# State-space SiLU as u/2 times (1 + tanh(u/2)), applied behind each convolution in a hybrid encoder step

## The chip, the cores and the metric

One Trainium2 chip; the kernel runs on one of its cores. The metric is device time in microseconds (us) of one launch, as the median of several runs. Engine names below: PE is TensorE (PEld its weight loads), DVE is VectorE, ACT is ScalarE, POOL is GpSimd, SP is SyncE.

## What is computed

One inference step of a hybrid encoder layer over 512 prompt frames and 64 sample frames, which the kernel handles together as T = 576 columns. The layer is a half SwiGLU feed-forward, a mixer, another half SwiGLU, and a final norm. The mixer has three branches: a state-space scan (SSD), band attention and an mLSTM. The change lies in the state-space branch:

```python
z, xbc, ... = split_cols(u @ lp['w_in'], IN_SIZES)
xbc, conv_new = causal_conv(xbc, conv_prev, lp['ssd_conv_w'], lp['ssd_conv_b'])   # width 4, per channel
xs, bm, cm = split_cols(jax.nn.silu(xbc), (SSD_WIDTH, SSD_GROUPS * SSD_STATE, SSD_GROUPS * SSD_STATE))
y, ssd_new = ssd_scan(xs, dt, a, bm, cm, h0)        # chunked scan, 16 heads in 4 groups
y = y + lp['ssd_d'][:, None] * xs
y_ssd = rmsnorm(y * jax.nn.silu(z), lp['ssd_norm'])
```

silu(v) is v times the logistic function of v. With u = v/2 it equals u times (1 + tanh(u)).

## The kernel before

Everything is kept with features on the 128 partitions and frames along the free axis. A matrix product is done in a split form (a rounded high part and a remainder, `ph` and `pl` for weights, `TH` and `TL` for activations; three products for one), with a seven-product scheme on 2 x 2 blocks: `stream` walks over blocks of weights, and each block gives seven products of 12 matmuls (`product`, L623). The weights come by DMA to `wr`, `wx` or are summed on POOL to `wy` (L479); `split` rounds them on ACT (L289, a cast) and takes the remainder on DVE (L290).

The mixer's projections run through `pairs`: two output tiles of 128 features at a time. A product's result lies in one of three accumulator banks; part of the results is first copied out by ACT to a temporary `uv` (L540), others are put in place by DVE together with a `uv` (L549), or by ACT alone (L547). A bank takes the next product only after that.

The mixer works in twelve units, `ORDER = a0 a1 m0 s0 a2 a3 s1 m1 s2 m2 s3 m3`: attention (a), mLSTM (m), state space (s). While the products of one unit stream through PE, the *job* of an earlier unit is woven in: each product calls `tick`, which advances a generator to its next `yield`. A unit's job is queued when its last product is done. So what a job emits is placed, in program order, among the products of the following unit. The order in which each engine finally issues its instructions isn't this order: a scheduler works it out from a simulated timeline, and each engine then runs its own list strictly in that order.

A state-space unit (`ssd_gemm`) has six tiles in three pairs: B and C, x0 and x1, z0 and z1. For B, C, x0, x1 the put function `conv` collects the two halves in a tile `raw` from a ring of four buffers (tag `P`, also used by attention and mLSTM jobs), copies three boundary columns out (L1156, L1157), and does the convolution: one ACT instruction (L1159, scale and bias) and three DVE instructions (L1162), into `acc` (a tile of tag `g`). z0 and z1 go to rows 0 and 1 of `R1`. The job (`ssd`) begins with its row loads by DMA (L182, L1182) and then applies the six SiLUs in a row (L1185, L1188), the first one before the others by `issue_after`. After that it multiplies B and C (L1197), turns B to frame-major order (`tok_major`, L906, L910) and x0, x1 likewise (L1226, L1230); x is weighted by `wd` on ACT (L1236), the decay matrices are formed on ACT (L1242 to L1245) and multiplied on POOL (L1246, L1247); then come the state chain and the outputs, the last with z (L1294, L1295).

ACT evaluates functions from a loaded table; the program has a table-load instruction (`ACT_TABLE_LOAD`) wherever a function is needed that the loaded set lacks. Exp and tanh are used all over the mixer, SiLU here and in the two feed-forwards.

Of the kernel before, what the change touches and what calls it, by code (L numbers as in the profile page):

```python
# [27 lines left out]
AF = mybir.ActivationFunctionType  # L28
ALU = mybir.AluOpType
# [29 lines left out]
C_CW = 48  # L59
C_CB = 112  # L60
# [21 lines left out]
class Hybrid:  # L82
# [1052 lines left out]
    def ssd_gemm(self, g):  # L1135
        nc = self.nc
        out = {}

        def conv(key, ct, col):
            box = {}  # L1140
            w = self.cst[:, C_CW + ct * 4:C_CW + ct * 4 + 4]

            def go(h, sl, emit):
                if not box:
                    box["raw"] = raw = self.P((128, 582))
                    nc.scalar.copy(raw[:, 0:3], self.zero)
                    nc.scalar.copy(raw[:, 515:518], self.cst[:, C_CS + ct * 3:C_CS + ct * 3 + 3])
                raw = box["raw"]
                m = min(sl.stop, TP)
                emit(raw[:, 3 + sl.start:3 + m], 0, m - sl.start)  # L1150
                if sl.stop > TP:
                    emit(raw[:, 6 + TP:6 + sl.stop], TP - sl.start, sl.stop - sl.start)
                box[h] = True
                if not (0 in box and 1 in box):
                    return
                nc.scalar.copy(self.co[:, ct, 0:3], raw[:, 512:515])  # L1156
                nc.scalar.copy(self.co[:, ct, 3:6], raw[:, 579:582])  # L1157
                acc = self.t("g", (128, 579))
                nc.scalar.activation(acc, raw[:, 0:579], AF.Identity, scale=w[:, 0:1],  # L1159
                                     bias=self.cst[:, C_CB + ct:C_CB + ct + 1])  # L1160
                for j in range(1, 4):
                    nc.vector.scalar_tensor_tensor(acc, raw[:, j:j + 579], w[:, j:j + 1], acc,  # L1162
                                                   op0=ALU.mult, op1=ALU.add)
                out[key] = acc
            return ("w_in", col), 1.0, go

        def zed(j, col):
            return ("w_in", col), 1.0, lambda h, sl, emit: emit(self.R1[:, j, sl])

        tiles = [conv("B", 8 + g, O_B + g * 128), conv("C", 12 + g, O_C + g * 128),  # L1170
                 conv("x0", 2 * g, O_X + g * 256), conv("x1", 2 * g + 1, O_X + g * 256 + 128),
                 zed(0, O_Z + g * 256), zed(1, O_Z + g * 256 + 128)]
        return tiles, out

    def ssd(self, g, t):
        nc = self.nc
        Bf, Cf = t["B"], t["C"]
# [4 lines left out]
                nc.scalar.dma_start(rows[j][2][r * 64:(r + 1) * 64, :], self.rows(4 * g + 2 * j + r, 64))  # L1182
        free = 2 + (self.b_i - 1) % 2 * 3

        last = nc.scalar.activation(self.R1[:, 0, :], self.R1[:, 0, :], AF.Silu)  # L1185
        with self.tc.issue_after(last.ins):
            for v in (Bf, Cf, t["x0"], t["x1"], self.R1[:, 1, :]):
                nc.scalar.activation(v, v, AF.Silu)  # L1188
        yield 2
        h4 = lambda ap: ap.rearrange("p c (h e) -> p c h e", e=64)  # L1190
        v4 = lambda ap: ap.rearrange("p (c t) -> p c t", t=128)
# [3 lines left out]
        for c in range(4):  # L1195
            sl = slice(c * 128, (c + 1) * 128)
# [10 lines left out]
        for j in range(2):  # L1207
# [7 lines left out]
            for r in range(2):  # L1215
                last = cum[r][:, 127:512:128]
# [37 lines left out]
            for c, (a, n) in enumerate(CH):  # L1254
# [9 lines left out]
                else:  # L1264
                    h = states[c]
                    for r in range(2):
                        hs = slice(r * 64, (r + 1) * 64)
                        nc.vector.scalar_tensor_tensor(new[:, hs], h[:, hs], el[:, c, r:r + 1], ps[:, hs],
                                                       op0=ALU.mult, op1=ALU.add)
# [73 lines left out]
    def merge(self):  # L1343
# [71 lines left out]
        half(1, (2, 3))  # L1415
        heads(7)
        ssd(range(2))
        half(2, (0, 1))
        ssd(range(2, 5))
        half(2, (2, 3))  # L1420
        ssd(range(5, 8))
        tiles = [(("w_proj_ssd", 0, 1024, n * 128, 128), [(0, put(n, 0))]) for n in range(8)]
        self.gemm(tiles[:4], ZH, ZL)
# [61 lines left out]

    def branches(self, x):
        nc = self.nc
        units = {"a": (self.attn_gemm, self.attn), "m": (self.ml_gemm, self.ml), "s": (self.ssd_gemm, self.ssd)}
        got = {u: units[u[0]][0](u[1]) for u in ORDER[:2]}
        with self.wide("m0"), self.pools("m0", xp=None, op=None):  # L1490
# [134 lines left out]
```

## Time and profile before

| | |
|---|---|
| runs | 1925.25, 1933.16, 1935.91 us; median 1933.16 |
| profiled execution (the page gives its span, and no other time for it) | 1934.5 us from the first to the last instruction |
| granted TensorE clock, mean | 0.992 |
| busy: PE, DVE, ACT, POOL | 97%, 79%, 56%, 35% of the span |
| table loads on ACT | 11 in all; 8 of them between 755 and 1147 us |

How to read it: the first feed-forward ends at about 550 us, the mixer lies between there and about 1365 us, and the second feed-forward fills the rest. The four state-space jobs begin at 755.7, 904.8, 1011.4 and 1116.9 us, where their first table load stands.

### The profile page before, as it was taken

What the parts mean: (1) busy time and instruction counts of PE and PEld (TensorE: products, weight loads), DVE (VectorE), ACT (ScalarE), POOL (GpSimd) and SP (SyncE); (2) the same over time, 40 slices, a digit from 0 to 9 for tenths busy, and PEclk for the clock granted to TensorE, in tenths of its full rate; (3) what the DMA queues carried; (4) which work ended last, traced back from release to release, by engine and by line L of the source; (5) the groups of instructions that cost most, each with busy time, mean ns of one, the idle gap of its engine ahead of it and who ended that gap; (6) DMA issues with size and microseconds to landing.
All of it is one profiled execution on the core that took longest, in us unless ns stands there. A gap on an engine that the chain in (4) does not pass through costs nothing. (4 is left out here: it accounts for less than half of the span.)

```text
span 1934.5 us, 37668 instructions
## 1 busy us (share of the span) xinstructions
PE 1884.4 (97%) x13901; PEld 1822.9 (94%) x13901; DVE 1525.9 (79%) x2715; ACT 1091.1 (56%) x2502; POOL 672.9 (35%) x644
## 2 busy tenths in 40 slices
PE   8999999999999999999999999999999999999998
PEld 8999999999999878888889989999999999999998
DVE  6999899988868767767777776745898988889765
ACT  5554654644534787767676766324565455554544
POOL 3433333333302234423535353450233333343311
PEclk9999999999999999999999999999999999999999
DMA  7266666666742545754666655672236666666631
GB/s 231 82 162 168 162 159 164 154 172 171 181 133 90 142 129 146 215 147 117 170 180 178 164 145 184 205 220 83 84 105 164 164 159 167 165 157 169 153 97 57
DMA packets 129439, 294.69 MB, mean 152 GB/s; under 512 B 14288, under 2 KB 26192, under 8 KB 129256
## 3 DMA queue, kind: packets, MB, share of 16 engines
q1 hardware_dynamic: 99496, 203.58, 32.5%
q0 software_dynamic: 20272, 74.20, 20.9%
q10 hardware_dynamic: 9488, 14.53, 2.5%
q8 instruction: 109, 1.79, 0.4%
q14 instruction: 74, 0.61, 0.1%
HBM read 272.87 MB, written 19.38 MB: 151 GB/s over the span
## 5 line engine op out<-in xcount | busy, mean ns | idle before, releaser
L623 PE MATMUL acc<-TH,ph 128*128 128x288 f32 x3220 | 966.7, 301 | 25.2 <-ACT uv L540 11.2
L623 PE MATMUL acc<-TL,ph 128*128 128x288 f32 x3220 | 954.1, 297 | 0.4 <-DVE TL L290 0.4
L623 PE MATMUL acc<-TH,pl 128*128 128x288 f32 x3220 | 952.5, 297 | 0.3 <-DVE pl L290 0.2
L623 PEld LDWEIGHTS acc<-TH,ph 128*128 128x128 f32 x3220 | 605.9, 188 | 45.2 <-ACT uv L540 14.7
L623 PEld LDWEIGHTS acc<-TL,ph 128*128 128x128 f32 x3220 | 607.3, 189 | 4.6 <-issue 3.7
L623 PEld LDWEIGHTS acc<-TH,pl 128*128 128x128 f32 x3220 | 606.6, 189 | 3.4 <-issue 2.0
L290 DVE TENSOR_TENSOR pl<-wr,ph 128x512 fp32r<-128x512 f32 x471 | 439.4, 940 | 89.1 <-ACT ph L289 76.8
L289 ACT CAST ph<-wr 128x512 fp32r<-128x512 f32 x471 | 286.7, 618 | 277.7 <-PE acc L623 140.7
L290 DVE TENSOR_TENSOR pl<-wx,ph 128x512 fp32r<-128x512 f32 x390 | 322.6, 831 | 38.8 <-ACT ph L289 32.6
L289 ACT CAST ph<-wx 128x512 fp32r<-128x512 f32 x390 | 236.9, 619 | 199.5 <-POOL wx L479 98.6
L479 POOL TENSOR_TENSOR wx<-wx,wr 128x512 f32<-128x512 f32 x160 | 243.6, 1522 | 181.7 <-DVE pl L290 147.0
L468 POOL DMA_DIRECT2D wx<-in_sblk x115 | 101.3, 898 | 504.8 <-DVE pl L290 156.8
L261 PE MATMUL acc<-YH,ph 128*128 128x256 f32 (+1 forms) x768 | 228.6, 299 | 2.5 <-ACT g L547 2.4
L261 PE MATMUL acc<-YL,ph 128*128 128x256 f32 (+1 forms) x768 | 229.0, 299 | 0.5
L261 PE MATMUL acc<-YH,pl 128*128 128x256 f32 (+1 forms) x768 | 229.3, 299 | 0.0
L261 PEld LDWEIGHTS acc<-YH,ph 128*128 128x128 f32 x768 | 147.0, 192 | 3.0 <-ACT g L547 2.6
L261 PEld LDWEIGHTS acc<-YL,ph 128*128 128x128 f32 x768 | 147.2, 192 | 1.6 <-DVE YL L340 1.5
L261 PEld LDWEIGHTS acc<-YH,pl 128*128 128x128 f32 x768 | 147.3, 192 | 0.0
L479 POOL TENSOR_TENSOR wy<-wx,wr 128x512 f32<-128x512 f32 x35 | 54.5, 1557 | 133.3 <-DVE pl L290 117.1
L662 DVE SCALAR_TENSOR_TENSOR R<-acc,R 128x288 f32<-128x288 f32 x168 | 75.5, 450 | 18.5 <-PE acc L623 17.9
L289 ACT CAST TH<-g 128x288 fp32r<-128x288 f32 x120 | 51.4, 434 | 54.8 <-POOL g L648 33.5
L290 DVE TENSOR_TENSOR pl<-wy,ph 128x512 fp32r<-128x512 f32 x70 | 61.3, 879 | 26.4 <-ACT ph L289 23.7
(321 smaller groups left out, 2386.4 us busy)
## 6 DMA issues: line engine op xcount, KB each, us to landing
wr<-in_sblk SPq DMA_DIRECT2D x345, 256.0 KB, 3.7
wx<-in_sblk POOLq DMA_DIRECT2D x119, 512.0 KB, 6.8
wx<-in_sblk SPq DMA_DIRECT2D x111, 512.0 KB, 3.8
wr<-in_wblk SPq DMA_DIRECT2D x126, 256.0 KB, 3.0
R<-scr_rows ACTq DMA_DIRECT2D x12, 576.0 KB, 5.7
gs<-g SPq DMA_DIRECT2D x20, 288.0 KB, 4.3
g<-gs POOLq DMA_DIRECT2D x20, 288.0 KB, 3.5
y<-ys POOLq DMA_DIRECT2D x12, 288.0 KB, 4.5
```

The lines of the kernel that those rows point to most:

```text
L261: nc.tensor.matmul(ps[:, :n], wt[:, wsl], xx[:, k0 + k, a:a + n], start=(k == 0 and i == 0), stop=(k == nk - 1 and i == 2))
L289: self.nc.scalar.copy(hi, src)
L290: self.nc.vector.tensor_tensor(lo, src, hi.bitcast(F32), op=ALU.subtract)
L468: return {"x12": x12, "src": src}, lambda: nc.gpsimd.dma_start(x12, src[:, 1:3, :], accum_op=ALU.add)
L479: add = lambda o, one, two: self.nc.gpsimd.tensor_tensor(o, one, two, op=ALU.add)
L623: self.nc.tensor.matmul(ps, wt[:, wsl], xx[:, kk, :], start=(start and kk == 0 and i == 0), stop=(kk == 3 and i == 2), skip_group_check=True)
L662: self.nc.vector.scalar_tensor_tensor(o, ps, scale, o, op0=ALU.mult, op1=ALU.add)
```

## The change

SiLU goes from ACT's SiLU function in the job to a tanh and one DVE instruction where the tile is finished. `silu_of_half(u, t)` writes tanh(u) to t (ACT, L1185 of the new file) and then u = (t + 1) * u (DVE, L1186). For B, C, x0, x1 it stands right behind the three convolution instructions and writes the tanh into `raw`, which stays taken so much longer. For z0 and z1 it stands behind the second half and takes a buffer of the `P` ring that was not taken before. The halving of u is put in the constants: one POOL instruction at the start of `branches` halves the convolution's weights and bias, and z's scale is 0.5 instead of 1.0. The six SiLUs of the job are gone.

```diff
                 for j in range(1, 4):
                     nc.vector.scalar_tensor_tensor(acc, raw[:, j:j + 579], w[:, j:j + 1], acc,
                                                    op0=ALU.mult, op1=ALU.add)
+                self.silu_of_half(acc, raw[:, 0:579])
                 out[key] = acc
...
         def zed(j, col):
-            return ("w_in", col), 1.0, lambda h, sl, emit: emit(self.R1[:, j, sl])
+            seen = []
+            def go(h, sl, emit):
+                emit(self.R1[:, j, sl])
+                seen.append(h)
+                if len(seen) == 2:
+                    self.silu_of_half(self.R1[:, j, :], self.P())
+            return ("w_in", col), 0.5, go
...
+    def silu_of_half(self, u, t):
+        self.nc.scalar.activation(t, u, AF.Tanh)
+        self.nc.vector.scalar_tensor_tensor(u, t, 1.0, u, op0=ALU.add, op1=ALU.mult)
...
-        last = nc.scalar.activation(self.R1[:, 0, :], self.R1[:, 0, :], AF.Silu)
-        with self.tc.issue_after(last.ins):
-            for v in (Bf, Cf, t["x0"], t["x1"], self.R1[:, 1, :]):
-                nc.scalar.activation(v, v, AF.Silu)
...
+        half = self.cst[:, C_CW:C_CB + 16]
+        nc.gpsimd.tensor_scalar(half, half, 0.5, None, op0=ALU.mult)
```

The table loads in the program fall from 11 to 3. Line numbers of the new file are 9 to 11 higher behind the change (L1197 becomes L1206, L1236 becomes L1245, L1242 to L1245 become L1251 to L1254). Since the scheduler orders each engine's list anew, instructions move in the whole stage. Three places show it.

ACT where unit s2's products end and its job begins, before (`ph<-wy` is a weight cast, `uv` and `R_60<-acc` empty accumulator banks):

```order
L289 CAST ph<-wy 128x512
L547 ACTIVATE R_60<-acc 128x288
L1185 ACT_TABLE_LOAD
L1185 ACTIVATE R_60<-R_60 128x576
L1188 ACTIVATE g<-g 128x579 x4
L1188 ACTIVATE R_60<-R_60 128x576
L289 CAST ph<-wy 128x512
L540 ACTIVATE uv<-acc 128x288 x2
```

The same place in the changed kernel; `P<-R_60` is the tanh of z1, and `t<-t,wd` is the weighting of x from the job itself:

```order
L547 ACTIVATE R_60<-acc 128x288
L551 ACTIVATE g<-g 128x288
L1185 ACTIVATE P<-R_60 128x576
L1146 COPY P<-zero 128x3
L1147 COPY P<-cst 128x3
L1245 ACTIVATE t<-t,wd 128x64 x8
L289 CAST ph<-wy 128x512
L1245 ACTIVATE t<-t,wd 64x64
L540 ACTIVATE uv<-acc 128x288 x2
```

The load and the six SiLUs between the bank copies L547 and `uv` are gone, and eight weighting instructions of the job, which stood behind the `uv` copies before, have moved up into their place.

ACT in the middle of unit s3's products, where a convolution (L1156 to L1159) meets the decay matrices of unit s2's job, before:

```order
L1157 COPY co<-P 128x3
L1159 ACTIVATE g<-P,cst 128x579
L1244 ACTIVATE R_60<-R_60 128x512
L289 CAST ph<-wy 128x512
L1245 ACTIVATE R_60<-R_60 64x64
L540 ACTIVATE uv<-acc 128x288 x2
L1244 ACTIVATE R_60<-R_60 128x512
```

And now (L1253, L1254 were L1244, L1245):

```order
L1251 ACTIVATE R_60<-R_60,TM 64x64
L1185 ACTIVATE P<-g 128x579
L289 CAST ph<-wy 128x512
L540 ACTIVATE uv<-acc 128x288 x2
L1253 ACTIVATE R_60<-R_60 128x512
L1254 ACTIVATE R_60<-R_60 64x64
L1253 ACTIVATE R_60<-R_60 128x512
L1159 ACTIVATE g<-P,cst 128x579
```

A tanh stands ahead of the `uv` copies, and the convolution and the decay matrices have moved behind them.

PE at the first matmuls of unit s2's job, before, with the engines that each one waits for:

```order
L623 MATMUL acc<-TH_7242,pl 128x288
L906 MATMUL ps_x<-ident,g 128x128 [waits PE_49,Activation_49]
L906 MATMUL ps_x<-ident,g 128x128 x3
L910 MATMUL ps_x<-ident,g 64x128
L1197 MATMUL ps_s<-g 128x128 [waits Activation_49]
L1197 MATMUL ps_s<-g 128x128 x3
L1201 MATMUL ps_s<-g 64x64
L623 MATMUL acc<-TH_7250,ph 128x288 [waits Activation_49]
```

And now (L1206, L1210 were L1197, L1201):

```order
L623 MATMUL acc<-TH_7250,pl 128x288
L1206 MATMUL ps_s<-g 128x128 [waits DVE_49]
L1206 MATMUL ps_s<-g 128x128 x3
L1210 MATMUL ps_s<-g 64x64
L906 MATMUL ps_x<-ident,g 128x128 x4
L910 MATMUL ps_x<-ident,g 64x128
L623 MATMUL acc<-TH_7244,ph 128x288 [waits DVE_49]
```

The job's first matmuls have moved 109 rows up in PE's list, about nine products, and what they wait for is DVE instead of ACT.

## The prediction

> **What bounds the kernel now.** I read the page's first part, then a table by stretches of time, then what PE waited for, and last the order of events around the SiLUs.
>
> ```profile
> PE 1884.4 (97%) x13901; PEld 1822.9 (94%) x13901; DVE 1525.9 (79%) x2715; ACT 1091.1 (56%) x2502; POOL 672.9 (35%) x644
> ```
>
> PE is busy for 1884.4 of 1934.5 us. No change of ACT's or DVE's work can take more from the time than PE's idle time, 50 us in all, unless PE's own work shrinks; the change leaves its matmuls alone. The stretch that the change touches is 700 to 1210 us; the first row is a quiet stretch of the feed-forward for comparison (columns: length, then busy time and count of PE, PEld, DVE, ACT, POOL, then granted clock, DMA share, GB/s).
>
> ```profile
> 300.00:400.00 100.00, 100.00 (x752) 99.94 (x751) 90.57 (x139) 55.19 (x116) 36.22 (x32) 1.00 0.62 161
> 700.00:1210.00 510.00, 488.93 (x3597) 448.70 (x3596) 366.55 (x735) 355.08 (x966) 203.42 (x204) 0.99 0.59 160
> ```
>
> In these 510 us PE is idle for 510 - 488.9 = 21.1 us. That is the ceiling of the gain here, and DVE, busy 366.6 us (72%), and ACT, 355.1 us (70%), both have room. What PE waited for in this stretch (total, times, longest):
>
> ```profile
> PE acc L623 <- ACT uv L540: 10.3, 10, 1.8
> PE acc L623 <- DVE g L549: 2.9, 2, 1.7
> PE acc L261 <- ACT g L547: 2.4, 1, 2.4
> PE acc L623 <- ACT g L547: 2.2, 3, 1.0
> PE acc L623 <- ACT R L547: 0.7, 1, 0.7
> PE ps_x L906 <- ACT g L1188: 0.6, 2, 0.3
> ```
>
> Most of it is an accumulator bank that ACT had not yet emptied (`uv` L540, L547); the SiLUs themselves (L1188) cost 0.6 us. So the SiLUs can matter through what is queued behind them on ACT. That is seen at the third state-space job (start, duration, engine, line; in brackets the idle time before and its releaser):
>
> ```profile
> 1010.92 0.40 ACT L547 ACTIVATE R<-acc 128x288 f32<-128x288 f32 x1
> 1011.35 1.28 ACT L1185 ACT_TABLE_LOAD   x1
> 1012.64 0.69 ACT L1185 ACTIVATE R<-R 128x576 f32<-128x576 f32 x1
> 1013.23 2.40 ACT L1188 ACTIVATE g<-g 128x579 f32<-128x579 f32 x4
> ...
> 1013.95 0.66 PE L906 MATMUL ps_x<-ident,g 128*128 128x128 f32 x4 [0.34 <-ACT g L1188]
> ...
> 1015.53 0.67 ACT L1188 ACTIVATE R<-R 128x576 f32<-128x576 f32 x1
> ...
> 1016.11 0.60 ACT L289 CAST ph<-wy 128x512 fp32r<-128x512 f32 x1
> ...
> 1016.62 0.69 ACT L540 ACTIVATE uv<-acc 128x288 f32<-128x288 f32 x2
> ...
> 1017.07 0.40 PE L623 MATMUL acc<-TH,ph 128*128 128x288 f32 x1 [1.12 <-ACT uv L540]
> ```
>
> From 1011.35 to 1016.2 us ACT does a table load and six SiLUs, then a weight cast, and only at 1016.62 the two `uv` copies. PE waits 0.34 us for the SiLU of B and 1.12 us for the bank. The other jobs show the same:
>
> ```profile
> 911.00 0.40 PE L623 MATMUL acc<-TH,ph 128*128 128x288 f32 x1 [0.90 <-ACT uv L540]
> ...
> 1119.52 0.66 PE L906 MATMUL ps_x<-ident,g 128*128 128x128 f32 x4 [0.30 <-ACT g L1188]
> ...
> 1122.63 0.40 PE L623 MATMUL acc<-TH,ph 128*128 128x288 f32 x1 [1.12 <-ACT uv L540]
> ```
>
> The first job, at 755.7 us, has no such wait behind it. A second kind follows later in each job, where exp needs its table back:
>
> ```profile
> 934.76 1.28 ACT L1074 ACT_TABLE_LOAD   x1
> ...
> 941.19 0.40 PE L623 MATMUL acc<-TH,ph 128*128 128x288 f32 x1 [0.99 <-ACT g L547]
> ...
> 1040.24 1.28 ACT L1074 ACT_TABLE_LOAD   x1
> ...
> 1046.15 0.40 PE L623 MATMUL acc<-TH,ph 128*128 128x288 f32 x1 [0.35 <-ACT g L547]
> ...
> 1145.81 1.28 ACT L1074 ACT_TABLE_LOAD   x1
> ...
> 1152.20 0.40 PE L623 MATMUL acc<-TH,ph 128*128 128x288 f32 x1 [0.82 <-ACT g L547]
> ```
>
> Between each of these loads and the bank copy that PE waits for some six microseconds later, ACT's rows follow each other without idle time; the load of 1.28 us is longer than each of the waits.
>
> **The change part by part.**
>
> *Loads and the row of SiLUs go.* The build has 3 loads instead of 11, so tanh shares exp's table. ACT loses 8 x 1.283 = 10.3 us of work, of which only what PE waited for is worth anything. Behind the row of SiLUs: 0.90 + 0.34 + 1.12 + 0.30 + 1.12 = 3.78 us. Behind the return to exp: 0.99 + 0.35 + 0.82 = 2.16 us. I count all of it, 5.94 us, as gone. From below it is worth 0: the eight weighting instructions of the job that now stand ahead of the `uv` copies can hold the bank just as long. From above it is all 13.8 us of the listed waits on ACT (10.3 + 2.2 + 0.7 + 0.6).
>
> ```profile
> L1162 DVE SCALAR_TENSOR_TENSOR g<-P,cst,g 128x579 f32<-128x579 f32 x48 | 44.0, 922 | 1.7 <-ACT g L1159 1.4
> ...
> L1162 DVE SCALAR_TENSOR_TENSOR g<-P,cst,g x48: 801/814/1824, 715.6 to 1110.0; 128x579 f32<-128x579 f32 x48
> ...
> L551 ACT ACTIVATE g<-g x44: 427/444/457, 657.4 to 1200.5; 128x288 f32<-128x288 f32 x44
> ...
> L1188 ACT ACTIVATE g<-g x16: 667/670/672, 757.5 to 1120.5; 128x579 f32<-128x579 f32 x16
> ...
> L1185 ACT ACT_TABLE_LOAD  x4: 1283/1283/1283, 755.7 to 1116.9; - x4
> ```
>
> Here the row and a rule differ. The Trainium skill, "ScalarE: Activation LUTs", section "What ACT_TABLE_LOAD costs", puts a switch at 1283 ns for the load and some 1380 ns for a drain. The load agrees; the drain isn't seen here: L547 ends at 1011.32, the load starts at 1011.35 and the SiLU at 1012.64. By the page 8 switches would free 21.3 us of ACT, an estimate, which would not change what PE waited for.
>
> *The tanhs.* 24 on ACT, in place of 24 SiLUs. Before, a SiLU over 128x579 took 0.670 us and a tanh over 128x288 (L551) 0.444 us, which is (0.670 - 0.444) / 291 = 0.78 ns per element for both together; so I take 0.67 us for a tanh and ACT's total stays. They move into the products' stretch, one at a time. Each waits for the convolution's third DVE instruction, and ACT's queue behind it holds casts and `uv` copies. If the scheduler placed it well it costs nothing; the cover is the copies' slack within one product. If DVE is late, ACT is late by as much. I count this in the next term.
>
> *24 new DVE instructions.* The nearest row is the convolution's own, L1162, the same kind on the same shape: 801 ns at the least, 814 in the median, with single ones up to 1824. At 0.814 to 0.922 us (the latter the group's mean) they are 19.5 to 22.1 us more, taking DVE from 72% to 76% of the stretch. PE waits on DVE there for 2.9 us in the listed rows. If these grow with busy over idle time, 366.6/143.4 = 2.56 to 388.7/121.3 = 3.20, they grow by a quarter: 0.7 us. From below 0, since no instruction of DVE's list got shorter; from above each could hold PE by its whole 0.81 us, 19.5 us.
>
> *PE waits on the new chain.* A job's first matmuls (L1206) now wait on DVE's last instruction for B and C, and stand some nine products earlier in PE's list than before. The nearest rows are the waits on L1188 that the old order left, 0.30 and 0.34 us: the scheduler places such a matmul just when it expects its input. I take 0.34 for each of four jobs, 1.4 us, with 0 below and, above, 1.84 us each (the longest wait on ACT, shown next): 7.4 us.
>
> *What a long wait costs besides.*
>
> ```profile
> 1095.04 0.40 PE L623 MATMUL acc<-TH,ph 128*128 128x288 f32 x1 [1.84 <-ACT uv L540]
> ```
>
> ```profile
> 1090.00:1095.00 5.00, 3.20 (x24) 1.00 0.57 173
> 1095.00:1100.00 5.00, 4.96 (x26) 0.66 0.01 3
> 790.00:795.00 5.00, 3.25 (x24) 1.00 0.14 49
> 795.00:800.00 5.00, 5.00 (x37) 1.00 0.70 197
> ```
>
> After the wait of 1.84 us the clock granted over the next 5 us is 0.66, that is 0.34 x 5 = 1.7 us more. After the wait of 790 to 795 us (1.75 us idle) it is 1.00. So a stall a little under 2 us may or may not cost as much again. None of the stalls that I count as gone is of this size, so no term for the clock.
>
> *The job moves up as a whole*, with its loads of decay rows on ACT's DMA queue, its stores on SP's and its products in POOL's list. ACT already waits for such loads:
>
> ```profile
> ACT el L1220 <- DMA R<-scr_rows: 9.6, 5, 3.6
> ```
>
> That wait moves along with the job; nothing makes the loads slower, so 0, with the 1.75 us idle of 790 to 795 us, where DVE waited for such a load too, as the price of one more bad meeting. SP's list differs by a few swapped places of stores and weight loads; no row of PE's waits above names a DMA, so 0 here as well.
>
> *Small parts.* The POOL instruction on 128x80 constants stands near the start of POOL's list, ahead of this one:
>
> ```profile
> 13.57 8.20 POOL L307 TENSOR_TENSOR sm<-sm,mhalf 128x2 f32<-128x2 f32 x1 [11.76 <-DVE sm L306]
> ```
>
> It lies in 11.76 us of idle time; even if it took a microsecond, nothing is queued behind it until 13.57. Its cost is 0; with that cover gone it would shift the first norm by its own length. z's tanhs write a `P` buffer and their DVE instructions are wanted only at the job's last POOL products: 0, hidden by the whole job. The `P` ring's buffers are held longer by one tanh and one DVE instruction, 0.67 + 0.81 = 1.5 us, while the fourth tile after it comes at least one pair, seven products, later: 7 x 12 matmuls x 0.133 us (100 us for 752, first row of the stretches) = 11.2 us. So 0; if the attention job in unit s1's stretch needed one sooner, ACT would stand for up to 1.5 us there, once.
>
> *The sum.* -5.94 + 0.7 + 1.4 = -3.8 us. Against the profiled execution's span: 1934.5 - 3.8 = 1930.7. The page gives no other time of that execution; the median run is 1.3 us below its span, so the forecast in the metric is 1933.2 - 3.8 = 1929.4, or 1929.
>
> **The rivals.** About 0.5%, 9.7 us, is what a measurement of this kernel can tell from no change (its own three runs lie 10.7 us apart).
>
> *Faster: ACT's relief reaches every bank copy.* The 1.84 us stall at 1095 us is no SiLU's: ahead of the `uv` copy stood a convolution and decay matrices, and the new order puts them behind it. If all 13.8 us of waits on ACT go, and the 1.7 us of clock, less 0.7 + 1.4: 1933.2 - 13.4 = 1920. For it: the new order at that place. Against it: several of the waits stand far from any SiLU. From 9.7 us on it counts as faster.
>
> *Slower: a tanh holds ACT's queue.* Place: the 16 tanhs behind convolutions. If the DVE instruction ahead is as late as L1162's slowest was, 1.824 - 0.814 = 1.01 us, ACT stands that long with the `uv` copies behind it; at all 16 that is 16.2 us, less the 5.94 gained, and with 0.7: 1933.2 + 11 = 1944. It decides from a mean of 1 us per tanh on, or from four stalls of 1.84 + 1.7 = 3.5 us on. For it: ACT runs strictly in order and the third DVE instruction stands between other work. Against it: the order shows a tanh mostly several instructions behind its convolution.
>
> *No change: the gain is paid back.* Weighting instructions and decay matrices, moved up with the job, take the place of the SiLUs ahead of the bank copies: 1933. For it: 8 x L1245 in the order at that place.
>
> *POOL kept waiting.* A new instruction reads two tiles in SBUF, as L1162 does, and the sums for weights on POOL read SBUF too:
>
> ```profile
> L479 POOL TENSOR_TENSOR wy<-wx,wr x35: 1258/1287/3742, 602.1 to 1167.3; 128x512 f32<-128x512 f32 x35
> ```
>
> One took 3742 ns against 1287 in the median, and L1162's slowest 1824 against 814, as if one stood for the other. POOL is busy 203.4 of 510 us, 40%; 40% of 19.5 us is 7.8 us of POOL made late, and if all of it reached PE: 1929.4 + 7.8 = 1937. Against it: no row of PE's waits in this stretch names POOL. The Trainium skill, "SBUF — State Buffer", section "Who interferes with whom", speaks against the change here: a DVE instruction with two inputs in SBUF and a GpSimd one that reads SBUF exclude each other for a whole instruction. By that rule the new instructions would make POOL late; the pair of 1824 and 3742 ns agrees with it.
>
> *It doesn't do what it says*, a load staying behind each tanh: the build has no such load, so 0.
>
> **How the numbers follow.** The forecast, 1929, with its own range of 1925 to 1932: 0.48. Paid back, 1933: 0.24. POOL, 1937: 0.06. Faster, 1920: 0.13. Slower, 1944: 0.09. The order is new for the whole stretch, and the spread of the runs comes on top; this leaves a little of the middle cases beyond 9.7 us. Faster by over 0.5%: 0.15; slower: 0.10; within: 0.75. The range reaches from the faster case, 1920, to short of the slower one, 1940: what is left out is the slower case, 0.09, and the part of the faster one below 1920, about 0.07: 0.16.
>
> **What would show it.** In the new profile: three load rows; no wait of 1.1 us behind a row of ACT functions at the four job starts; 24 new DVE rows at 0.8 to 0.9 us; PE idle between 700 and 1210 us of 16 to 18 us instead of 21.1. A first matmul of a job that waits over 1 us for DVE would show the chain mis-sized; ACT idle ahead of a tanh and then a `uv` wait would show the slower rival. Wrong it would be, above all, if PE's idle time falls or rises by over 10 us from the new order alone.

## The result, and the profile after

The changed kernel takes 1953.44 us in the median (1951.31 to 1955.99, 4 runs) against 1933.18 us beside it (1925.25 to 1935.91, 4 runs): a ratio of 1.0111 with a 95% interval of 1.0084 to 1.0139. That is 20 us more, where 4 us less was forecast, and the two groups of runs are 15 us apart at their nearest. The profiled execution of it has a span of 1950.4 us and took 1952.16 us.

The first part of the page, and the table by stretches (columns as in the prediction). Its second row is one of the new stalls and its third what follows it:

```profile
PE 1888.3 (97%) x13901; PEld 1825.2 (94%) x13901; DVE 1540.1 (79%) x2739; ACT 1080.4 (55%) x2494; POOL 668.5 (34%) x645
```

```profile
700.00:1210.00 510.00, 478.27 (x3485) 441.08 (x3485) 373.72 (x736) 331.79 (x925) 195.54 (x195) 0.97 0.56 152
1010.00:1015.00 5.00, 1.80 (x7) 1.80 (x8) 5.00 (x7) 1.03 (x2) 1.55 (x3) 0.70 0.20 53
1015.00:1020.00 5.00, 5.00 (x28) 5.00 (x27) 3.73 (x7) 2.24 (x6) 0.88 (x1) 0.62 0.71 196
```

The build did what it was to do: ACT is busy 10.7 us less than before (1080.4 against 1091.1), and the load rows in the jobs are gone. But PE is busy 478.3 of the 510 us instead of 488.9. It stands idle 31.7 us instead of 21.1, and the granted clock of the stretch falls from 0.99 to 0.97. What PE waited for there:

```profile
PE acc L623 <- DVE R L549: 12.0, 4, 4.8
PE acc L623 <- ACT g L547: 7.0, 4, 3.4
PE ps_x L1126 <- DVE Q L1120: 6.0, 2, 3.2
PE acc L623 <- DVE g L549: 3.4, 2, 2.9
PE ps_x L1235 <- DVE t L912: 1.3, 1, 1.3
PE acc L623 <- ACT uv L540: 0.7, 2, 0.5
```

The `uv` waits of 10.3 us, the largest of the waits in the forecast, are down to 0.7; e1 below shows that this is the new order's doing and not the loads'. In their place stand 12.0 us behind a DVE bank copy of z (`R` L549) that no row of before showed, with 4.8 us at the longest, 7.0 us behind the last bank copies of ACT (2.2 before), and 6.0 us behind the mLSTM job's normalisation (L1120). The place of the longest is the end of unit s2's products (start, duration, engine, line; only DVE, POOL and the waits):

```profile
1002.19 5.30 POOL L1255 TENSOR_TENSOR R<-R,t 128x512 f32<-128x512 f32 x3
...
1004.55 1.78 DVE L290 TENSOR_TENSOR pl<-wy,ph 128x512 fp32r<-128x512 f32 x1
1006.25 1.86 DVE L1162 SCALAR_TENSOR_TENSOR g<-P,cst,g 128x579 f32<-128x579 f32 x1
...
1007.44 1.40 POOL L1256 TENSOR_TENSOR R<-R,t 64x64 f32<-64x64 f32 x3
1008.03 4.14 DVE L1186 SCALAR_TENSOR_TENSOR g<-P,g 128x579 f32<-128x579 f32 x1
...
1008.81 1.25 POOL L1255 TENSOR_TENSOR R<-R,t 128x512 f32<-128x512 f32 x1
1010.03 0.31 POOL L1256 TENSOR_TENSOR R<-R,t 64x64 f32<-64x64 f32 x1
1010.30 1.25 POOL L479 TENSOR_TENSOR wy<-wy,wr 128x512 f32<-128x512 f32 x1
...
1012.10 0.68 DVE L290 TENSOR_TENSOR pl<-wx,ph 128x512 fp32r<-128x512 f32 x1
...
1012.70 0.45 DVE L549 SCALAR_TENSOR_TENSOR R<-acc,uv 128x288 f32<-128x288 f32 x1
1013.07 0.81 DVE L1162 SCALAR_TENSOR_TENSOR g<-P,cst,g 128x579 f32<-128x579 f32 x1
...
1013.20 0.61 PE L623 MATMUL acc<-TH,ph 128*128 128x288 f32 x1 [4.83 <-DVE R L549]
...
1013.97 0.69 ACT L1185 ACTIVATE P<-g 128x579 f32<-128x579 f32 x1 [6.68 <-DVE g L1162]
...
1015.36 0.76 DVE L1186 SCALAR_TENSOR_TENSOR g<-P,g 128x579 f32<-128x579 f32 x1
```

POOL starts the decay products of the job (L1255, L1256, the old L1246, L1247) at 1002.19 us and goes on with one instruction behind another until 1011.5. DVE's rows beside it are stretched: a weight remainder L290 takes 1.78 us instead of the 0.68 of 1012.10, L1162 takes 1.86 instead of 0.81, and the new L1186 takes 4.14 us. The 0.76 us of 1015.36 is what L1186 takes when POOL is still. The bank copy L549 is queued behind them on DVE, PE behind the bank copy for 4.83 us, and ACT's tanh behind the last L1162 for 6.68 us. The next longest of these waits, 4.58 us at 1129.98, has the same burst ahead of it; there a weight remainder L290 took 4.08 us. The windows show the price of it twice: 3.2 us of idle PE in 1010 to 1015 us, and a clock of 0.70 there and 0.62 in the next 5 us, together 0.30 x 1.80 + 0.38 x 5.00 = 2.4 us more of PE's busy time.

The groups of the rows concerned (count, then the least, the median and the longest duration in ns):

```profile
L1162 DVE SCALAR_TENSOR_TENSOR g<-P,cst,g x48: 801/817/2630, 709.8 to 1129.8; 128x579 f32<-128x579 f32 x48
...
L1186 DVE SCALAR_TENSOR_TENSOR g<-P,g x16: 743/755/4145, 716.9 to 1132.1; 128x579 f32<-128x579 f32 x16
L1186 DVE SCALAR_TENSOR_TENSOR R<-P,R x8: 739/746/1653, 746.7 to 1137.5; 128x576 f32<-128x576 f32 x8
```

L1186 is the size that was forecast, 0.755 us in the median; what was not forecast is its longest. In before the same POOL instructions began at 1016.49 us, when DVE's bank copies of unit s2 were done. DVE's longer rows beside them were two weight remainders, and the first bank copy of the next unit came at 1019.96:

```profile
1006.70 0.44 DVE L549 SCALAR_TENSOR_TENSOR R<-acc,uv 128x288 f32<-128x288 f32 x1
...
1016.49 6.43 POOL L1246 TENSOR_TENSOR R<-R,t 128x512 f32<-128x512 f32 x4 [3.37 <-DVE t L1198]
...
1016.74 1.58 DVE L290 TENSOR_TENSOR pl<-wy,ph 128x512 fp32r<-128x512 f32 x1
...
1018.25 1.79 DVE L290 TENSOR_TENSOR pl<-wx,ph 128x512 fp32r<-128x512 f32 x1
```

The six SiLUs no longer stand at the job's head, and so the scheduler moved the job up. The forecast had seen this on PE's list and priced it there; it had not followed the same move down to POOL's list, where it puts the products among the convolutions.

### The profile page after: what moved, and what is told of

Same layout as the page of the kernel before. It is cut to its first block, busy times and chain, and to the rows that moved or that the text cites. A ratio compares the mean times of both kernels' runs of the same rounds, so it can differ in the third digit from the quotient of the medians.

```text
span 1950.4 us, 37679 instructions
## 1 busy us (share of the span) xinstructions
PE 1888.3 (97%) x13901; PEld 1825.2 (94%) x13901; DVE 1540.1 (79%) x2739; ACT 1080.4 (55%) x2494; POOL 668.5 (34%) x645
## 5 line engine op out<-in xcount | busy, mean ns | idle before, releaser
L290 DVE TENSOR_TENSOR pl<-wr,ph 128x512 fp32r<-128x512 f32 x471 | 431.4, 921 | 85.4 <-ACT ph L289 72.9
L290 DVE TENSOR_TENSOR pl<-wx,ph 128x512 fp32r<-128x512 f32 x390 | 319.3, 822 | 32.7 <-ACT ph L289 26.7
L479 POOL TENSOR_TENSOR wx<-wx,wr 128x512 f32<-128x512 f32 x160 | 243.6, 1522 | 173.1 <-DVE pl L290 138.3
L479 POOL TENSOR_TENSOR wy<-wx,wr 128x512 f32<-128x512 f32 x35 | 49.8, 1424 | 130.0 <-DVE pl L290 105.8
L290 DVE TENSOR_TENSOR TL<-g,TH 128x288 fp32r<-128x288 f32 x120 | 55.9, 469 | 25.7 <-ACT TH L289 25.7
```

The costliest lines, as they stand in the source:

```text
L290: self.nc.vector.tensor_tensor(lo, src, hi.bitcast(F32), op=ALU.subtract)
L479: add = lambda o, one, two: self.nc.gpsimd.tensor_tensor(o, one, two, op=ALU.add)
```

## The experiments

All times are compared with the kernel before, run beside them on the same chip (its medians there were 1932.45 us for e1 to e4, 1931.52 for e5 to e8, 1929.05 for e9 to e13 and 1931.6 for e14 to e16). The last column is the ratio less 1, times 1933 us; by it the changed kernel stands at +21.5. The ratio can differ by some 2 us from that of the two medians. e1, e4, e5, e9 and e14 to e16 leave out a part of the result or put tanh for SiLU.

| run | what differs | median us | ratio to before (95%) | us |
|---|---|---|---|---|
| e1 | before, tanh for SiLU | 1922.49 | 0.9952 (0.9930 to 0.9973) | -9.3 |
| e2 | changed, job's matmuls held back | 1935.67 | 1.0019 (1.0003 to 1.0035) | +3.7 |
| e3 | all of it at the job's start | 1937.64 | 1.0022 (1.0008 to 1.0037) | +4.3 |
| e4 | changed, no DVE instruction | 1937.37 | 1.0025 (1.0005 to 1.0044) | +4.8 |
| e5 | changed, no POOL products | 1931.22 | 0.9998 (0.9984 to 1.0011) | -0.4 |
| e6 | changed, products a little later | 1939.5 | 1.0034 (1.0018 to 1.0050) | +6.6 |
| e7 | e2, z on ACT and POOL | 1945.92 | 1.0072 (1.0055 to 1.0089) | +13.9 |
| e8 | before, an early pow on POOL | 1931.45 | 1.0001 (0.9984 to 1.0018) | +0.2 |
| e9 | before, no POOL products | 1923.3 | 0.9965 (0.9947 to 0.9982) | -6.8 |
| e10 | e2, products a little later | 1928.53 | 1.0000 (0.9985 to 1.0015) | 0.0 |
| e12 | changed, products a step later | 1926.71 | 0.9998 (0.9981 to 1.0015) | -0.4 |
| e13 | e2, products a step later | 1933.11 | 1.0016 (1.0002 to 1.0030) | +3.1 |
| e14 | e4, no POOL products | 1926.99 | 0.9986 (0.9966 to 1.0007) | -2.7 |
| e15 | e2, no POOL products | 1930.0 | 0.9991 (0.9978 to 1.0003) | -1.7 |
| e16 | e1, no POOL products | 1920.95 | 0.9954 (0.9930 to 0.9978) | -8.9 |

**e1: the loads alone.** Only the function's name changes, so the eight loads are gone and no instruction moves on any engine.

```diff
-        last = nc.scalar.activation(self.R1[:, 0, :], self.R1[:, 0, :], AF.Silu)
+        last = nc.scalar.activation(self.R1[:, 0, :], self.R1[:, 0, :], AF.Tanh)
...
-                nc.scalar.activation(v, v, AF.Silu)
+                nc.scalar.activation(v, v, AF.Tanh)
```

> The kernel before with the six SiLU functions of each state-space job replaced by tanh in the same place, nothing else (the result is tanh, not SiLU). It takes away the eight table loads and leaves every other instruction as before. Theory 'order' (the job, freed from the row of SiLUs, starts some 15 us earlier and its POOL products meet the convolutions on DVE), theory 'DVE load' (the 24 new instructions) and theory 'ACT queue' (tanhs behind convolutions hold ACT) all expect a gain here, by the stalls that the loads caused: about 1927 us, -3 to -6. Same or slower would mean that the loads were worth nothing.

Measured 9.3 us less, with an interval of 5.2 to 13.5 us, where 3 to 6 were expected. The 5.94 us of the forecast lie inside it, but the trace gives less. PE's list is the same in both kernels, so its waits can be compared one by one: of the eight waits that the forecast added up, four are gone and four are still there at 0.44 to 0.48 us, so 4.1 of the 5.94 us went. Over the stretch's rows PE's idle time falls from 21.0 to 17.3 us, and the `uv` waits hardly change (10.3 before):

```profile
PE acc L623 <- ACT uv L540: 8.9, 9, 2.3
```

Five of the eight runs lie at 1919 to 1923 us and three at 1931 to 1933, and the cause of this spread is open (e8). The same step without POOL's products, from e9 to e16, gains only 2 us. So the loads are worth something between 2 and 9 us; these runs don't tell more closely.

**e2: the job held back.** The changed kernel, with B times C, its last piece and the turning of B queued on PE behind the last product matmul of z0.

```diff
+        with self.tc.issue_after(t["gate"]):
             for c in range(4):
...
+        with self.tc.issue_after(t["gate"]):
             nc.tensor.matmul(ps[:64, :64], Bf[:, 515:], Cf[:, 515:], start=True, stop=True)
```

> The changed kernel with one addition: PE's first matmuls of each state-space job (the product of B and C, the turn of B) are queued behind the last product of z0, where the kernel before held the job by its row of SiLUs. All 24 tanhs and 24 DVE instructions stay. Theory 'order': the loss goes, 1925 to 1936 us, and the single waits of PE over 3 us before a job's start vanish. Theories 'DVE load' and 'ACT queue': still slow, 1945 to 1955.

It takes back 17.8 of the 21.5 us. So the order, not the 24 instructions as such, made most of the loss. POOL's products come later with it; of the new rows only z's still stand beside them (1581 ns in the mean, against 859 in the changed kernel), and PE's waits on `R` L549 are down:

```profile
L1187 DVE SCALAR_TENSOR_TENSOR R<-P,R 128x576 f32<-128x576 f32 x8 | 12.6, 1581 | 0.2 <-ACT P L1186 0.2
```

```profile
PE acc L623 <- DVE R L549: 1.8, 3, 0.8
```

One row makes this mean. It took 6.02 us beside six POOL instructions, longer than any of the stretched rows above, and yet PE's wait for the bank copy behind it was only 1.35 us. (The profiled execution of e2, 1924.68 us, is the fastest of its eleven runs.)

```profile
751.07 6.02 DVE L1187 SCALAR_TENSOR_TENSOR R<-P,R 128x576 f32<-128x576 f32 x1
...
758.12 0.40 PE L623 MATMUL acc<-TH,ph 128*128 128x288 f32 x1 [1.35 <-DVE g L549]
```

**e3: the instructions without the new place.** The tanhs and the DVE instructions all stand at the job's start, where the SiLUs were; the halves are in the constants.

```diff
-                nc.scalar.activation(v, v, AF.Silu)
+                th = self.P((128, 582))[:, :n]
+                nc.scalar.activation(th, v, AF.Tanh)
+                nc.vector.scalar_tensor_tensor(v, th, 1.0, v, op0=ALU.add, op1=ALU.mult)
```

> The new formula in the old place: tanh and the DVE instruction for all six tiles at the job's start, constants halved as in the change. Same 24 tanhs, same 24 DVE instructions, no table loads. Theory 'order': 1928 to 1938 us. Theory 'DVE load': 1945 to 1955. Theory 'ACT queue' (the harm is in the convolutions' stretch): 1928 to 1938.

13.6 us above e1, at the upper edge of what two of the theories expect and below that of DVE's load. The scheduler's list shifts with it, so this is not the price of the 24 instructions alone.

**e4: the new place without the DVE instructions.** The tanh is written in place (y is that of tanh).

```diff
-        self.nc.scalar.activation(t, u, AF.Tanh)
-        self.nc.vector.scalar_tensor_tensor(u, t, 1.0, u, op0=ALU.add, op1=ALU.mult)
+        self.nc.scalar.activation(u, u, AF.Tanh)
```

> The changed kernel without the new DVE instruction: the tanh is applied in place behind each convolution and z (the result is tanh, not SiLU). The job starts as early as in the changed kernel. Theory 'order': still slow, 1942 to 1953 us, with PE waits over 2 us around the job's start. Theory 'DVE load': back to 1925 to 1933. Theory 'ACT queue': still slow, with ACT idle ahead of tanhs.

It came out between the two: 14.1 us above e1 and 16.7 below the changed kernel. Neither the theory of order alone nor that of DVE's load alone holds. Without the 24 instructions the scheduler also places many other rows differently, so the 16.7 us aren't their price alone. Up to here it was not shown what in the order does it.

**e5: the products left out.** In the changed kernel the 32 POOL instructions are dropped. Every other engine's list is the same, row for row.

```diff
-                nc.gpsimd.tensor_tensor(e[:, :512], e[:, :512], cb[:, :512], op=ALU.mult)
-                nc.gpsimd.tensor_tensor(e[:64, 512:], e[:64, 512:], cb[:64, 512:], op=ALU.mult)
```

> The changed kernel without POOL's 32 products of the decay matrices with C.B (their result is left out of y); every other engine has the same list. Theory (POOL's burst of products holds DVE's rows back, and the bank copy of z with them): the DVE rows of 1.8 and 4.1 us beside the burst come down to 0.8 to 0.9 us, PE's 12.0 us of waits on DVE's R at L549 go nearly to 0, and with them some 8 of the 17 us of lost clock: 1930 to 1938 us. Rival (the early job costs PE by its own matmuls and by DVE's longer list, wherever POOL stands): 1945 to 1953 us, with the waits on R still there.

21.9 us less than the changed kernel: the whole loss. PE's stretch and its waits in this run:

```profile
700.00:1210.00 510.00, 489.99 (x3591) 452.95 (x3591) 361.28 (x757) 342.54 (x941) 175.33 (x176) 0.98 0.59 162
```

```profile
PE acc L623 <- ACT g L547: 5.8, 3, 2.6
PE ps_x L1126 <- DVE Q L1120: 5.3, 2, 3.0
...
PE acc L623 <- DVE R L549: 0.6, 1, 0.6
```

The waits on `R` are gone. The other two stalls of the changed kernel, 7.0 and 6.0 us there, are nearly as they were, so they aren't the products'. In every run for which the scheduler made a new list (e2 to e7, e10 to e15) they come to 3.1 to 7.8 and 2.5 to 6.9 us; the one behind L1120 is in none with the old list (before, e1, e8, e9, e16). The `uv` waits are the other way round, 8.9 to 11.0 us with the old list and at most 3.6 with a new one, but for e7. Which rows of the new order bring the two stalls wasn't followed.

PE is busy 490.0 of the 510 us, more than before's 488.9. What the products took from DVE is seen in the groups of the same counts, of the changed kernel and then of this run (columns: busy us, mean ns, idle time ahead):

```profile
L290 DVE TENSOR_TENSOR pl<-wx,ph 128x512 fp32r<-128x512 f32 x61 | 52.8, 866 | 8.7 <-ACT ph L289 7.9
L290 DVE TENSOR_TENSOR pl<-wy,ph 128x512 fp32r<-128x512 f32 x60 | 52.2, 872 | 13.9 <-ACT ph L289 12.1 <-issue 1.8
L1162 DVE SCALAR_TENSOR_TENSOR g<-P,cst,g 128x579 f32<-128x579 f32 x48 | 50.5, 1055 | 1.1 <-ACT g L1159 0.8
L1186 DVE SCALAR_TENSOR_TENSOR g<-P,g 128x579 f32<-128x579 f32 x16 | 18.2, 1136 | 0.1
```

```profile
L290 DVE TENSOR_TENSOR pl<-wx,ph 128x512 fp32r<-128x512 f32 x61 | 47.4, 777 | 8.7 <-ACT ph L289 7.8
L290 DVE TENSOR_TENSOR pl<-wy,ph 128x512 fp32r<-128x512 f32 x60 | 43.5, 727 | 15.1 <-ACT ph L289 13.3 <-issue 1.8
L1162 DVE SCALAR_TENSOR_TENSOR g<-P,cst,g 128x579 f32<-128x579 f32 x48 | 44.8, 938 | 1.1 <-ACT g L1159 0.8
L1186 DVE SCALAR_TENSOR_TENSOR g<-P,g 128x579 f32<-128x579 f32 x16 | 14.6, 911 | 0.5 <-ACT P L1185 0.4
```

The weight remainders L290 gain 5.4 + 8.7 us, L1162 gains 5.7 and L1186 3.6 by the deletion: 23.4 us of DVE, for 668.5 - 638.6 = 29.9 us of POOL's work taken away. Over the whole page DVE is busy 20.4 us less (1540.1 and 1519.7). Single rows of L1162 and L1186 up to 2.6 and 1.8 us remain; the weight sums L479 are still there.

**e9: the control.** The same deletion in the kernel before; again no other row moves.

> The kernel before without POOL's 32 products of the decay matrices with C.B (their result is left out of y), all else in the same order. Theory (the products cost only where they meet a unit's last convolutions): in before's order they stand behind these, so little is gained, 0 to 5 us: 1927 to 1932 us against some 1932. Rival (the products cost DVE as much wherever they stand, and the 22 us that leaving them out of the changed kernel gained says nothing of the place): 1910 to 1918 us.

It gains 6.8 us, interval 3.5 to 10.2, a little above the theory's 5 and far from the rival's 15 and more. So the 32 products cost 6.8 us in the old order and 21.9 us in the new one. The difference of 15.1 us, with some 7 to either side, belongs to the new order around them; that it is their own place in POOL's list, e6 shows. The rows agree: in the old order the products hardly stretch the convolutions (the kernel before, then e9):

```profile
L290 DVE TENSOR_TENSOR pl<-wr,ph 128x512 fp32r<-128x512 f32 x98 | 77.2, 796 | 19.1 <-ACT ph L289 17.4 <-PE ps_v L1006 0.7
L1162 DVE SCALAR_TENSOR_TENSOR g<-P,cst,g 128x579 f32<-128x579 f32 x48 | 44.0, 922 | 1.7 <-ACT g L1159 1.4
```

```profile
L290 DVE TENSOR_TENSOR pl<-wr,ph 128x512 fp32r<-128x512 f32 x100 | 72.5, 733 | 18.0 <-ACT ph L289 16.1 <-PE ps_v L1006 0.7
L1162 DVE SCALAR_TENSOR_TENSOR g<-P,cst,g 128x579 f32<-128x579 f32 x48 | 43.1, 901 | 2.7 <-ACT g L1159 2.4
```

L1162 gives back 0.9 us, and what DVE lost was mostly weight remainders, (796 - 733) ns x 98 = 6.2 us in the group shown. On the page DVE is busy 13.1 us less (1525.9 and 1512.8), so the old order's products stretched it too, by two thirds of e5's 20.4 us, but cost a third of the time. That a late remainder finds more slack ahead of PE than a late bank copy is what the times suggest; it wasn't tried by itself.

**e6: only POOL moves.** The products stay, each queued behind the weight sum that was written last in program order, which puts them one or two sums later in POOL's list; on the other engines only two neighbouring DVE rows change places, one of them a memset.

```diff
+                with self.tc.issue_after(self.pl.ins):
                     nc.gpsimd.tensor_tensor(e[:, :512], e[:, :512], cb[:, :512], op=ALU.mult)
```

> The changed kernel with the same 32 products put one or two weight sums later in POOL's list and nothing else moved on any engine. Theory (it is the meeting of the burst with z's convolution stretch on DVE that costs): the waits on R at L549 shrink from 12.0 us to under 6, time 1935 to 1948 us, unless the later products hold the job's own matmuls. Rival (place of the products is no matter): 1950 to 1956 us.

14.9 us less by moving these POOL instructions alone. PE's waits on `R` (L550 in this file) are 0.8 us instead of 12.0 and no longer among its larger ones, and the longest new row falls from 4145 ns to 2208:

```profile
PE acc L624 <- ACT g L548: 7.1, 3, 3.0
PE ps_x L1127 <- DVE Q L1121: 6.3, 2, 3.2
PE acc L624 <- DVE g L550: 3.8, 5, 1.3
```

```profile
L1187 DVE SCALAR_TENSOR_TENSOR g<-P,g x16: 743/764/1837, 714.3 to 1119.7; 128x579 f32<-128x579 f32 x16
L1187 DVE SCALAR_TENSOR_TENSOR R<-P,R x8: 742/746/2208, 742.5 to 1124.1; 128x576 f32<-128x576 f32 x8
```

**e10, e12, e13: how far the repair goes.** e10 is e2 with the products later as in e6; e12 is the changed kernel, and e13 is e2, with each head's products written one `yield` later and queued behind a weight sum as well. In e12 and e13 the scheduler's list shifts on the other engines too.

> The gate run (1935.7 us; the job's first matmuls held back) with POOL's products one or two weight sums later on top, nothing else moved. Theory (what the gate run still lost was the meeting of the products with z's DVE rows, 1.58 us each there against 0.86): z's rows at 0.8 to 1.1 us, 1928 to 1934 us. Rival (what is left is DVE's longer list as such): 1935 to 1939 us.

> The changed kernel with the products one step of the job later still than in the run that only put them later (1939.5 us); the planned order of the other engines shifts with it. Theory (clear of the unit's convolutions the early job is harmless): 1930 to 1937 us. Rival (the early job costs by itself, or PE now waits for the products): 1938 to 1945 us, with waits on POOL's products at L1291 in the second case.

> The held-back job and the products a step later. Theory (no meeting is left): the best of the versions with all 24 instructions, 1926 to 1932 us, so faster than before or the same. Rival (DVE's 24 instructions cost 10 us wherever POOL stands): 1934 to 1940 us.

e10 and e12 come out level with the kernel before, e12 below the range of its theory, and e13 3.1 us above the kernel before and so between its theory and its rival. In e10 z's new rows are down from 1581 to 1104 ns in the mean, as expected. In e12 the new rows are as long as in the run without products (890 and 860 ns in the mean against 911 and 859). None of the versions that compute the whole result is faster than before beyond its interval. Holding back twice (e13) gained nothing over holding back once; what it costs was not followed further.

**e14, e15, e16: what the rest goes to.** The runs e4, e2 and e1 without the products.

> The early job without the 24 DVE instructions (1937.4 us with the products) and without POOL's products (both parts of the result left out). Theory (the early job costs only by the products that come early with it): 1916 to 1923 us. Rival (it also costs by itself, by job matmuls that wait among the unit's products): 1927 to 1934 us, no better than the changed kernel without products (1931.2).

> The held-back job with the 24 DVE instructions (1935.7 us with the products), without POOL's products. Theory (the 24 instructions cost some 9 us by themselves, as between the run of tanh alone and the best with all parts): 1926 to 1932 us. Rival (they cost only where POOL's products meet them): 1916 to 1922 us.

> Only the function changed, in the old place (1922.5 us with the products), without POOL's products. Every theory: as in the kernel before, where leaving them out gained 6 us: 1915 to 1919 us. If it gains 15 us or more, the products cost in the old order too and the place is not what matters.

With e1, e2, e4, e5 and the changed kernel they make a table (us against before). Each entry has 2.4 to 5.3 us to either side, and each difference 4 to 6.

| | products in | products out | what the products cost |
|---|---|---|---|
| old list, tanhs in the job (e1, e16) | -9.3 | -8.9 | about 0 |
| tanhs behind the convolutions, job held back, 24 DVE instructions (e2, e15) | +3.7 | -1.7 | 5 |
| tanhs behind the convolutions, early job, no DVE instruction (e4, e14) | +4.8 | -2.7 | 8 |
| tanhs behind the convolutions, early job, 24 DVE instructions (changed, e5) | +21.5 | -0.4 | 22 |

Along a row POOL's list alone differs, but for a DVE memset and its neighbour in the first three. Down a column the scheduler's lists differ in many rows, so a step down isn't the price of the named thing alone.

Without the products the three lower rows stand 7, 6 and 8.5 us above the first, which is about what e1 had gained; the two stalls that stay in e5 are found in all three. With the products they stand 13.0, 14.1 and 30.8 us above it. e14 came out at 1926.99 us, above its theory (1916 to 1923) and at the edge of its rival (1927 to 1934), so the early job, or the list that comes with it, does cost a little by itself. e15 agreed with its theory; e16 gained nothing on e1 where 6 us were expected. The products cost next to nothing in the first row and 22 us in the last. e9 and e16 give 6.8 and about 0 for the same deletion in one order, which shows how far such differences can be trusted.

**e7: z's part off DVE.** The held-back job with z's sum on ACT and its product on POOL.

```diff
+            self.nc.scalar.activation(t, t, AF.Copy, bias=1.0)
+            eng.tensor_tensor(u, t, u, op=ALU.mult)
```

> The held-back job (as in the gate run, 1935.7 us) with z's part taken off DVE: one more ACT copy that adds 1, and the product on POOL, 8 of each. Theory (what is left of the loss is DVE's 24 instructions): a third of them gone, 1928 to 1934 us. Rival (z's instructions had cover, and POOL's product shuts DVE out as before): 1934 to 1940 us.

Worse than either theory: 10.2 us above e2. PE's largest wait there is on ACT's `uv` copies, 13.8 us, 6.4 at the longest. Which of the two added instructions delays these copies wasn't separated.

**e8: the spread of the runs.** The kernel before, with one pow over 128 x 1 right behind the constant's memset.

```diff
+        one = c.tile([128, 1], F32, name="warm", tag="warm")
+        nc.gpsimd.memset(one, 1.0)
+        nc.gpsimd.tensor_tensor(one, one, self.mhalf, op=ALU.pow)
```

> The kernel before with one pow on POOL over 128x1 right at its start, besides the first one at 13.6 us, which took 8.20 us in the profile of before and 1.70 us in the others. Theory (the 6.5 us between these is what parts the runs of before into about 1925 and about 1933): nearly all runs at 1924 to 1928 us, first norm's pow 0.1 to 1.7 us. Rival (the two groups have another cause): groups stay, median 1931 to 1934 us.

The spread stays (1925.74 to 1937.27 us), and the first norm's pow takes 1.70 us in the one execution profiled. An early pow doesn't take the spread away, and its cause stays open.

## Why the prediction was wrong

*What held.* The load rows are gone from the jobs, and taking them out alone gains: e1 measures 9.3 us (5.2 to 13.5) where 5.94 was summed from the waits. That the two numbers agree is in part luck, since only 4.1 of the 5.94 us went in e1's trace. The fall of the `uv` waits to 0.7 us came with the new order, not with the loads.

*The step that failed first* was "The job moves up as a whole, with its loads of decay rows on ACT's DMA queue, its stores on SP's and its products in POOL's list", which was costed for the loads and for SP, and for the products at nothing. They are the 15.1 us by which e5 gains more than e9, and e6, which moves these POOL instructions alone, gains 14.9. The order of POOL would have shown it: the products had moved from behind the unit's bank copies to among its convolutions.

*The step that failed next* was the term of 0.7 us for 24 DVE instructions. Busy over idle time was the wrong scale, since it takes DVE's rows as given and lets only their number grow. The runs put the step at 7 us without POOL's products (e15 against e16), 13.0 with them in the held-back order (e2 against e1), and 16.7 in the early order (changed against e4). Each has 5 to 7 us to either side and the shift of the other rows in it, so the price of the instructions alone isn't shown, but all three lie above 0.7. The upper end of 19.5 us in the text would have covered them; the value taken was at the wrong end.

*The term of 1.4 us for PE's waits on the new chain* was no worse than too large: PE has no wait at the first matmuls L1206 in this execution, and 1.7 us further down the chain (1.3 at L1235 and 0.4 at L910). But the early job, with the list that comes with it, stood 6 us above e1's order without products and 14.1 with them (e4 against e1). The stalls behind L547 and L1120, 7.0 and 6.0 us, had no term at all. The sign that the forecast had named for itself came: PE's idle time in the stretch rose by 10.6 us, from 21.1 to 31.7.

*The clock* was given no term, since none of the stalls counted as gone was long. The stalls that came were longer. Over windows of 5 us from 600 to 1230 us, PE's idle time is 41.1 us after and 26.7 before, and its busy time times (1 - granted clock) is 14.9 us after and 7.6 before. The two rise by 21.7 us together, a third of it by the clock.

*The rivals.* "POOL kept waiting" named the right pair of engines and the wrong loser, with 1937 us and a chance of 0.06. The Trainium skill, "SBUF — State Buffer", section "Who interferes with whom", has such pairs exclude each other; the trace agrees, with 4.14 us for a DVE row of 0.755. The forecast took it that POOL would stand for DVE, though its own row of 1824 against 814 ns, beside a weight sum of POOL of 1785, was DVE standing for POOL. "The gain is paid back" is what is left without the products (e5, -0.4 us), by other rows than it named. "A tanh holds ACT's queue" gave the right sign, 1944 us, and the sign it named was there too: ACT stood 21.9 us ahead of the tanhs, five times. It was an effect: behind the stretched L1162 rows, and e5, with the same tanhs in the same order, has 6.1 us of it:

```profile
ACT P L1185 <- DVE g L1162: 21.9, 5, 6.7
```

```profile
ACT P L1185 <- DVE g L1162: 6.1, 5, 3.2
```

## What to carry to other kernels

Where a change lets a piece of work start earlier, follow the move on every engine's list, down to the one that seems to have time, and ask what runs beside it there. A second look at the longest rows of a group, 1.8 us where the median is 0.8, tells which engines stand for each other. A burst on one engine can hold a row of the other for its whole length; what that costs depends on what is queued behind that row. When an experiment must tell which engine is to blame, drop one engine's rows so that all the other lists stay the same, and do the same in the kernel before: only the difference of the two is the place's.

## What the runs showed of the hardware

- A DVE instruction beside a burst of POOL instructions doesn't lose one turn but several: L1186 ran from 1008.03 to 1012.17 us while POOL finished its L1256, did one more L1255 and L1256, and a weight sum L479 that ended at 1011.55. It takes 0.743 us at the least. In e2 an L1187 took 6.02 us beside six POOL instructions. The Trainium skill, "SBUF — State Buffer", section "Who interferes with whom", calls the pair of ports that the two engines share an exclusive lock, with issue order deciding who blocks. The trace agrees that DVE stood, and shows besides that the one that stood was not served next.
- It goes the other way as well: in before a weight sum L479 took 3.74 us at 1002.49 (1.28 when alone) while DVE ran L1162 and L290 rows.
- Each of PE's seven waits of 2.78 us and more between 600 and 1230 us of the changed kernel left a window of 5 us at 0.52 to 0.81 of the clock (0.62 behind the 4.83 us, 0.52 behind one of 4.58); those of 2.24 us at 802 and of 2.01 us at 903 us left it at 1.00, though before's 1.84 us had brought 0.66. The length of a wait alone doesn't tell.
- The first pow on POOL (L307, 128 x 2 at 13.6 us) took 8.20 us in the profiles of before and of e16 and 1.70 in all others; the mixer starts 4 to 8 us later there (554.4 and 554.6 us against 546.5 to 550.7). All kernels with the POOL instruction on the constants, which runs ahead of it, have 1.70, but so have e1, e8 and e9 without it. What makes the difference is not shown.
